# Two layers of a hybrid attention and mLSTM block on one core: another way to make the low parts of the mixers' weight pieces

## The chip, the core and the metric

The kernel runs on one core of a Trainium2 chip. The core has TensorE (matrix products), VectorE, ScalarE, GpSimd and SyncE, each with its own queue of instructions that it takes in order, and 16 DMA engines that all queues share. The metric is the device time of one execution in microseconds, as a median of several runs.

## What is computed

Two layers, each a mixer and a feed-forward part over 512 positions of width 1024. The mixer projects the normalized input to eight groups of columns, runs dilated attention on three of them and a bidirectional mLSTM on the others, and projects the result back. Everything is float32.

```python
def hybrid_mixer(hn, w_in, mlstm_conv_w, mlstm_conv_b, mlstm_gate_b, mlstm_head_g, w_out):
    ...
    aq, ak, av, mq, mk, mv, mo, gates = jnp.split(hn @ w_in, split_at, axis=-1)
    ...
    attn = dilated_attention(q, k, v)
    ...
    qk = jax.nn.silu(depthwise_conv_centred(jnp.concatenate([mq, mk], axis=-1), mlstm_conv_w, mlstm_conv_b))
    ...
    h_fwd = mlstm_direction(q, k, v, g[0], jax.nn.log_sigmoid(g[1]))
    h_bwd = flip(mlstm_direction(flip(q), flip(k), flip(v), flip(g[2]), flip(jax.nn.log_sigmoid(g[3]))))
    ...
    return jnp.concatenate([attn, mlstm], axis=-1) @ w_out

def reference(x, ...):
    for l in range(DEPTH):
        mixed = hybrid_mixer(rms_norm(x, mix_pre_g[l]), w_in[l], ...)
        x = x + rms_norm(mixed, mix_post_g[l])
        ff = conv_ffn(rms_norm(x, ffn_pre_g[l]), w_up[l], ...)
        x = x + rms_norm(ff, ffn_post_g[l])
    return x
```

## The kernel before

**Products in three parts.** A large product is not made in plain float32. Both operands are split into a high part, rounded to float32r, and a low part, the rest. Each product is then a triple of matmuls: high weight by high input, low weight by high input, high weight by low input (`mac`, lines 230 to 232). Where the weights move through the array instead (the V columns), the triple stands in lines 923 to 925.

**Pieces.** The weights come in pieces of 128 x 8 x 128 numbers, 512 KB. A layer has 104: 28 of `w_in` (numbered 0 to 27 here), 8 of `w_out`, 44 of `w_up`, 24 of `w_down`. `plan` lists them in the order of use. `load_raw` lets SyncE load the next piece into one of three raw buffers (`RAW`). `split_w` then makes the two parts in the next buffers of two rings of three (`RING`): line 183 lets ScalarE write the high part `whi`, and `lo_part` (line 115) lets VectorE subtract it from the raw piece and write the low part `wlo`; then the next load is issued. Some pieces get other places (`alloc`), those of `w_in` never. A buffer of a ring is free when TensorE has read the piece three before for the last time. `prefetch` splits up to two pieces ahead of the one in use.

**Rounds of the mixer.** `w_in` is worked off in four rounds and a tail; `ORDER` gives the letters of each round: q and k are the mLSTM's projections, a and b the attention's, V a pair of pieces for the V columns of both, used together by `proj_v` (first sister for four of eight blocks, the second for the other four, for each of four chunks of positions). The pieces are: round one q 0, k 1, a 2, V 3 and 4, b 5; round two a 6, q 7, b 8, k 9, V 10 and 11; round three q 12, k 13, V 14 and 15, a 16, b 17; round four q 18, a 19, b 20, k 21, V 22 and 23; tail 24 to 27. Between the matmuls of the projections, two streams interleave the steps of attention (`attn`) and of the mLSTM (`mlstm`): scores on TensorE, a maximum on VectorE (line 749), exp and scaling on ScalarE (752, 754), transposes on TensorE (760), the split of the transposed weights on ScalarE and VectorE (763, 115), the product with V (786).

**What sets the order.** The program is written in one order, and a scheduler then orders the instructions of each engine by its own estimates of when each can start. A change of one instruction thus moves others.

At the start of a mixer the scale of the rows is made (`scale_ready`): VectorE computes it, TensorE spreads it, ScalarE copies it to `prow` (line 394), VectorE multiplies the tables (`tb`, 538 and 539) and the first projections (`cu`, 664) by it.

Of the kernel before, what the change touches and what calls it, by code (L numbers as in the profile page):

```python
# [11 lines left out]
AF = mybir.ActivationFunctionType  # L12
ALU = mybir.AluOpType
# [12 lines left out]
RAW = 3  # L26
LINE = 256
RING = 3
HD = 128
KSC = HD ** -0.5  # L30
SUM1, ROW1, SUM2, ROW2 = [int(t * 2400) for t in (0.6, 3.3, 2, 8)]
# [50 lines left out]
def tile_hybrid_block(ctx: ExitStack, tc: tile.TileContext, xt, w_in, w_g, w_out, w_up, w_down, par, cst, out):  # L82
    nc = tc.nc
# [6 lines left out]
    base = const  # L90
    wraw_p, whi_p, wlo_p = Lines(big, small, RAW), Lines(big, small, RING), Lines(big, small, RING)
    pp = pool("pp", space=PSUM)
# [21 lines left out]
    def lo_part(dst, src, hi):  # L114
        nc.vector.tensor_tensor(out=dst, in0=src, in1=f32v(hi), op=ALU.subtract)  # L115
# [50 lines left out]
    def split_w(alloc=None):  # L166

        if not raw_q:
            return None
        raw, nk, i = raw_q.popleft()  # L170
        parts = {}
        n = 8
        k = 0
        while k < nk:
            if alloc is None:

                o = 16 if i in moving else 0
                hi, lo = (q.tile([P, 8 * P + LINE // 4], F32R, tag=t, name=t)[:, o:o + 8 * P].rearrange("p (k c) -> p k c", k=8)
                          for q, t in ((whi_p, "whi"), (wlo_p, "wlo")))
            else:  # L180
                hi, lo, n = alloc()
            m = min(n, nk - k)
            nc.scalar.copy(out=hi[:, 0:m, :], in_=raw[:, k:k + m, :])  # L183
            lo_part(lo[:, 0:m, :], raw[:, k:k + m, :], hi[:, 0:m, :])
            for j in range(m):
                parts[k + j] = (hi[:, j, :], lo[:, j, :])
            parts["all"] = (hi, lo)
            k += m
        load_raw()
        return parts  # L190
# [285 lines left out]
    def mixer_first(l, xp, sp, G, more, whole=False):  # L476
# [23 lines left out]
        if more:  # L500
            scale.go(1)
            w = take()
            prefetch(RING - 1)
            ps = s_ps()
# [6 lines left out]
    def mixer(l, xp, first, mp, post):  # L511
# [377 lines left out]

        prefetch(RING - 1)  # L890
        scale_ready()
# [5 lines left out]
        def proj():  # L897
            if pss:
                return pss.pop(0)
            w = take()  # L900
            prefetch(RING - 1)
            ps = mm_ps()
# [102 lines left out]
        for m in range(G):  # L1005
            mac(pss[m], ws[m], order[7], cp[order[7]], False, True)
        prefetch(RING)
        for m in range(G):
# [6 lines left out]
        for m in range(G, KT - 2):  # L1015
            w = take()
            ps = o_ps() if m == G else mm_ps()
            prefetch(RING if m == G else RING - 1)
            for n, k in enumerate(order):
# [262 lines left out]
```

## Time and profile before

| | us |
|---|---|
| median of 3 runs (1354.68 to 1354.85) | 1354.69 |
| the profiled execution | 1353.89 |
| its span in the profile | 1352.0 |
| first mixer, from the start of the span | about 25 to 262 |
| second mixer | about 697 to 930 |

The profile is of one execution; its span runs from the first to the last instruction, and the rest of its 1353.89 us lies around it. Times in its rows are from the start of the span. A row of a timeline gives start, duration, engine, line, operation, output and inputs, and in brackets idle time before it with what ended that. In a table by stretch each engine's busy time stands with its number of instructions.

### The profile page before, as it was taken

To read this page: it belongs to the slowest core of one execution; us is meant where nothing else is said; L and a number is where in the kernel's file an instruction comes from. 1 tells how busy PE (TensorE), PEld (TensorE's weight loads), DVE (VectorE), ACT (ScalarE), POOL (GpSimd) and SP (SyncE) were. 2 spreads that over 40 slices of the span, in tenths; PEclk is the share of its full clock that TensorE was granted. 3 is DMA by queue.
4 is the path that set the end of the run, shared out by engine and by line. 5 is a ranking of instruction groups with operands and counts; after the bars stand their busy time and mean duration, and the time that the engine had idled before them with its cause. 6 is when DMAs were issued, how large, how long until landed. Compare 5 with 4: busy or idle time off the path is not lost.

```text
span 1352.0 us, 18666 instructions
## 1 busy us (share of the span) xinstructions
PE 1323.9 (98%) x7152; PEld 1128.6 (83%) x7152; DVE 954.0 (71%) x1901; ACT 713.1 (53%) x1218; POOL 85.3 (6%) x100
## 2 busy tenths in 40 slices
PE   7999999999999999999989999999999999999996
PEld 5888878899888888888978898888998888888886
DVE  6999798847887777422499988887569777773233
ACT  5686696654544444323347867966446444443220
POOL 0000000024000000001130000000320000000002
PEclk9999999999999999999999999999999999999998
DMA  6212112231233332333321122123213333333321
GB/s 238 63 41 86 47 48 79 78 126 44 68 107 96 104 97 90 90 97 111 96 85 51 60 64 65 45 79 99 90 47 96 106 95 94 94 96 96 98 86 63
DMA packets 34089, 115.34 MB, mean 85 GB/s; under 512 B 3664, under 2 KB 6352, under 8 KB 34000
## 3 DMA queue, kind: packets, MB, share of 16 engines
q1 hardware_dynamic: 34000, 114.15, 27.9%
q8 instruction: 56, 0.92, 0.3%
q14 instruction: 33, 0.27, 0.1%
HBM read 112.04 MB, written 2.10 MB: 84 GB/s over the span
## 4 chain that ended last, share of the span: by engine, by line
PE 85%; DVE 7%; ACT 7%; issue 1%; DMA 0%; POOL 0%; SPq 0%; ACTq 0%; DVEq 0%
PE mm L230 18%; PE mm L232 18%; PE mm L231 18%; PE o L230 5%; PE o L231 5%; PE o L232 5%; PE mm L924 2%; PE mm L925 2%; PE mm L923 2%; PE o L786 2%; ACT rb L707 1%; PE t L760 1%; PE t L344 1%; DVE wlo L115 1%; ACT p L752 1%; PE s L743 1%
## 5 line engine op out<-in xcount | busy, mean ns | idle before, releaser
L115 DVE TENSOR_TENSOR wlo<-wraw,whi 128x1024 fp32r<-128x1024 f32 (+1 forms) x192 | 236.5, 1234 | 175.4 <-ACT whi L183 173.3
L230 PE MATMUL mm<-ah,whi 128*128 128x512 f32 (+1 forms) x880 | 337.0, 383 | 0.0
L232 PE MATMUL mm<-al,whi 128*128 128x512 f32 (+1 forms) x880 | 333.2, 380 | 0.8 <-DVE al L378 0.7
L231 PE MATMUL mm<-ah,wlo 128*128 128x512 f32 (+1 forms) x880 | 333.3, 379 | 0.0
L183 ACT CAST whi<-wraw 128x1024 fp32r<-128x1024 f32 (+1 forms) x192 | 198.0, 1035 | 163.2 <-PE mm L232 112.3
L232 PEld LDWEIGHTS mm<-al,whi 128*128 128x128 f32 x880 | 166.2, 189 | 30.8 <-DVE al L378 1.6
L230 PEld LDWEIGHTS mm<-ah,whi 128*128 128x128 f32 x880 | 166.5, 189 | 28.8 <-ACT whi L183 0.5
L231 PEld LDWEIGHTS mm<-ah,wlo 128*128 128x128 f32 x880 | 166.6, 189 | 27.3
L326 POOL TENSOR_TENSOR acc<-acc,sq 128x512 f32<-128x512 f32 x22 | 29.5, 1342 | 1127.0 <-ACT sq L323 1122.6
L230 PE MATMUL mm<-hh,whi 128*128 128x512 f32 x220 | 85.6, 389 | 0.0
L231 PE MATMUL mm<-hh,wlo 128*128 128x512 f32 x220 | 85.6, 389 | 0.0
L232 PE MATMUL mm<-hl,whi 128*128 128x512 f32 x220 | 85.6, 389 | 0.0
L1059 DVE TENSOR_TENSOR u<-mm,prow 128x512 f32<-128x512 f32 x64 | 43.8, 687 | 50.0 <-PE mm L232 39.6
L1076 ACT CAST hh<-cv 128x512 fp32r<-128x512 f32 x44 | 27.3, 620 | 87.6 <-DVE cv L1073 87.6
L923 PE MATMUL mm<-whi,ah 128*128 128x256 f32 x256 | 72.4, 284 | 0.9 <-DVE cu L664 0.9
L924 PE MATMUL mm<-wlo,ah 128*128 128x256 f32 x256 | 71.7, 280 | 0.4 <-DVE wlo L115 0.4
L925 PE MATMUL mm<-whi,al 128*128 128x256 f32 x256 | 71.4, 279 | 0.0
L1071 ACT ACTIVATE cg<-cg 128x512 f32<-128x512 f32 x44 | 27.8, 632 | 74.6 <-DVE cg L1065 74.3
L231 PE MATMUL o<-ah,wlo 128*128 128x512 f32 (+1 forms) x160 | 60.6, 379 | 0.0
L232 PE MATMUL o<-al,whi 128*128 128x512 f32 (+1 forms) x160 | 60.5, 378 | 0.0
L230 PE MATMUL o<-ah,whi 128*128 128x512 f32 (+1 forms) x160 | 60.5, 378 | 0.0
L752 ACT ACTIVATE p<-p,mx 128x512 f32<-128x512 f32 x64 | 46.2, 722 | 18.2 <-DVE mx L749 16.9
(319 smaller groups left out, 2754.9 us busy)
## 6 DMA issues: line engine op xcount, KB each, us to landing
wraw<-in_w_up SPq DMA_DIRECT2D x88, 512.0 KB, 3.6
wraw<-in_w_in SPq DMA_DIRECT2D x56, 512.0 KB, 3.6
wraw<-in_w_down SPq DMA_DIRECT2D x32, 512.0 KB, 3.5
wraw<-in_w_out SPq DMA_DIRECT2D x16, 512.0 KB, 3.6
wraw<-in_w_down SPq DMA_DIRECT2D x16, 384.0 KB, 3.1
x<-in_xt SPq DMA_DIRECT2D x4, 512.0 KB, 7.3
out_dram<-x SPq DMA_DIRECT2D x8, 256.0 KB, 2.1
tb<-in_cst SPq DMA_DIRECT2D x2, 967.0 KB, 5.4
```

The lines of the kernel that those rows point to most:

```text
L115: nc.vector.tensor_tensor(out=dst, in0=src, in1=f32v(hi), op=ALU.subtract)
L183: nc.scalar.copy(out=hi[:, 0:m, :], in_=raw[:, k:k + m, :])
L230: nc.tensor.matmul(out=ps, lhsT=hi, rhs=rh, start=first, stop=False)
L231: nc.tensor.matmul(out=ps, lhsT=lo, rhs=rh, start=False, stop=False)
L232: clock[1] = nc.tensor.matmul(out=ps, lhsT=hi, rhs=rl, start=False, stop=last).ins
L326: e.tensor_tensor(out=self.acc[:, cols], in0=self.acc[:, cols], in1=sq, op=ALU.add)
L752: nc.scalar.activation(out=p_, in_=p_, func=AF.Exp, scale=-1.0, bias=mx, accum_out=den)
L923: nc.tensor.matmul(out=o_, lhsT=xh, rhs=hi, start=(k == 0), stop=False)
L924: nc.tensor.matmul(out=o_, lhsT=xh, rhs=lo, start=False, stop=False)
L925: clock[1] = nc.tensor.matmul(out=o_, lhsT=xl, rhs=hi, start=False, stop=(k == KT - 1)).ins
L1059: nc.vector.tensor_tensor(out=u, in0=ps, in1=st["row"], op=ALU.mult)
L1071: nc.scalar.activation(out=g, in_=g, func=AF.Gelu_apprx_tanh)
```

## The change

For 52 pieces, those of `w_in` in both layers without the first four of layer 0, the low part is made in another way: ScalarE writes minus the raw piece, rounded like the high part, into the buffer of the low part (line 187 of the new code), and then GpSimd issues a DMA (188) that reads the raw piece and the buffer, adds them and writes the sum to the buffer. VectorE has no part in it. The write needs the raw piece and the free buffer, not the high part, so it may stand ahead of the cast. All other pieces are split as before. What waited for VectorE's subtraction (TensorE's second matmul, the next load into the raw buffer) now waits for the DMA's landing.

```diff
@@ -26,6 +26,7 @@
 RAW = 3
 LINE = 256
 RING = 3
+PIECES = 104
 HD = 128
...
             m = min(n, nk - k)
             nc.scalar.copy(out=hi[:, 0:m, :], in_=raw[:, k:k + m, :])
-            lo_part(lo[:, 0:m, :], raw[:, k:k + m, :], hi[:, 0:m, :])
+            if alloc is None and i % PIECES < 28 and i > 3:
+
+                nc.scalar.activation(out=lo[:, 0:m, :], in_=raw[:, k:k + m, :], func=AF.Copy, scale=-1.0)
+                nc.gpsimd.dma_start(out=lo[:, 0:m, :], in_=raw[:, k:k + m, :], accum_op=ALU.add)
+            else:
+                lo_part(lo[:, 0:m, :], raw[:, k:k + m, :], hi[:, 0:m, :])
             for j in range(m):
```

Lines from 188 on lie 6 higher in the new code: L713 there is L707 here. The numbers behind names are those of buffers and differ between the two programs.

**ScalarE, fourth round of layer 0.** `whi_8619` before and `whi_8666` now are piece 23. Before:

```order
L763 CAST pth_8509<-t_8511 128x4x128
L752 ACTIVATE p_8502,den_8505<-p_8502,mx_8503 128x512
L707 COPY rb_8603<-mm_8556 32x512
L183 CAST whi_8619<-wraw_8219 128x1024
L754 ACTIVATE p_8502<-p_8502,den_8505 128x512
L183 CAST whi_8661<-wraw_8327 128x1024
L763 CAST pth_8509<-t_8518 128x4x128
L886 COPY cat6_8594<-t_8589 128x512
```

Now:

```order
L769 CAST pth_8555<-t_8564 128x4x128
L892 COPY cat6_8641<-t_8636 128x512
L713 COPY rb_8650<-mm_8603 32x512 x3
L796 COPY cat2_8280<-o_8536 64x512
L184 CAST whi_8666<-wraw_8264 128x1024
L187 ACTIVATE wlo_8667<-wraw_8264 128x1024
L184 CAST whi_8709<-wraw_8373 128x1024
L673 ACTIVATE ca_8700<-cu_8698,par1_67 128x512
```

The cast now stands behind the last attention copies, which stood behind it, and the write of minus the raw piece follows it. From the cast of piece 20 to that of piece 23, ScalarE has 51 instructions between before and 58 now: three writes of minus the raw piece, one L754, one L763, one L790 and one L886 more.

**TensorE, the V pair 22 and 23 of layer 0.** `wlo_8551` and `wlo_8620` before are the low parts of 22 and 23, `wlo_8597` and `wlo_8667` now; `mm` is the chunk pair's sum. Before:

```order
L923 MATMUL mm_8667<-whi_8550,ah_6248 128x256
L924 MATMUL mm_8667<-wlo_8551,ah_6248 128x256
L786 MATMUL o_8490<-pth_8509,vs_8062 128x256 x4
L925 MATMUL mm_8667<-whi_8550,al_6249 128x256
L923 MATMUL mm_8667<-whi_8619,ah_6257 128x256
L924 MATMUL mm_8667<-wlo_8620,ah_6257 128x256
```

Now:

```order
L931 MATMUL mm_8716<-whi_8596,al_6276 128x256
L929 MATMUL mm_8716<-whi_8666,ah_6284 128x256
L929 MATMUL mm_8765<-whi_8596,ah_6250 128x256
L930 MATMUL mm_8765<-wlo_8597,ah_6250 128x256
L931 MATMUL mm_8765<-whi_8596,al_6251 128x256
L929 MATMUL mm_8765<-whi_8596,ah_6257 128x256
```

and, eight rows on,

```order
L931 MATMUL mm_8765<-whi_8596,al_6276 128x256
L929 MATMUL mm_8765<-whi_8666,ah_6284 128x256
L236 MATMUL mm_8838<-ah_6250,whi_8709 128x512
L930 MATMUL mm_8716<-wlo_8667,ah_6284 128x256
L931 MATMUL mm_8716<-whi_8666,al_6285 128x256
```

The first use of the low part of 23 now stands behind all four triples of the second chunk with piece 22, one more high-part matmul and the first matmul of piece 24.

**VectorE, start of the mixer of layer 1.** `wlo_6628` is the low part of piece 4; that of piece 3 stands four rows ahead of the rows shown. Before:

```order
L115 TENSOR_TENSOR wlo_6628<-wraw_6061,whi_6627 128x1024
L296 SCALAR_TENSOR_TENSOR rs_y_6588<-rs_a_6589,rs_y_6588 128x2
L551 TENSOR_TENSOR G_6647<-t_6642,G_6647 128x64
L395 TENSOR_SCALAR rt_6329<-rs_y_6588 128x2
L552 TENSOR_TENSOR G_6647<-G_6647,rt_6329 128x64
```

Now:

```order
L302 SCALAR_TENSOR_TENSOR rs_y_6616<-rs_a_6617,rs_y_6616 128x2
L530 CAST bdm_6588<-tb_6584 64x512
L401 TENSOR_SCALAR rt_6356<-rs_y_6616 128x2
L544 TENSOR_TENSOR tb_6584<-tb_6584,prow_6357 128x512
L545 TENSOR_TENSOR tb_6584<-tb_6584,prow_6357 128x512
L670 TENSOR_TENSOR cu_6633<-mm_6354,prow_6357 128x512
```

Both subtractions are gone, and the work on the gates (`G`) stands behind the tables and `cu`.

## Rows read from the trace of the kernel before

**Rows 1.** Page, busy time of each engine: us, share of the span, instructions.

```profile
PE 1323.9 (98%) x7152; PEld 1128.6 (83%) x7152; DVE 954.0 (71%) x1901; ACT 713.1 (53%) x1218; POOL 85.3 (6%) x100
```

**Rows 2.** Busy time in both mixers: length, PE, PEld, DVE, ACT, POOL, clock, DMA, GB/s.

```profile
25.00:262.00 237.00, 233.92 (x1428) 201.21 (x1428) 211.64 (x535) 172.77 (x340) 0.13 (x1) 1.00 0.22 63
697.00:930.00 233.00, 230.46 (x1413) 198.14 (x1412) 209.61 (x520) 171.49 (x339) 0.00 (x0) 1.00 0.22 64
```

**Rows 3.** TensorE's waits in both mixers: total us, times, longest.

```profile
PE s L864 <- DVE r L871: 0.7, 1, 0.7
PE s L864 <- DVE hs L874: 0.5, 1, 0.5
PE t L760 <- ACT p L754: 0.4, 2, 0.2
...
PE mm L923 <- DVE cu L664: 0.9, 1, 0.9
PE s L743 <- DVE mx L749: 0.3, 1, 0.3
```

**Rows 4.** First mixer by line: busy us, mean ns, idle before, what ended it.

```profile
L115 DVE TENSOR_TENSOR wlo<-wraw,whi 128x1024 fp32r<-128x1024 f32 x28 | 34.2, 1221 | 3.4 <-ACT whi L183 3.3
...
L183 ACT CAST whi<-wraw 128x1024 fp32r<-128x1024 f32 x28 | 29.1, 1046 | 9.1 <-PE mm L925 4.8 <-PE mm L232 4.2
```

**Rows 5.** Timelines of VectorE and TensorE at the start of layer 1's mixer.

```profile
699.21 1.22 DVE L115 TENSOR_TENSOR wlo<-wraw,whi 128x1024 fp32r<-128x1024 f32 x1
...
702.98 1.28 DVE L664 TENSOR_TENSOR cu<-mm,prow 128x512 f32<-128x512 f32 x2
...
703.81 0.36 PE L923 MATMUL mm<-whi,ah 128*128 128x256 f32 x1 [0.86 <-DVE cu L664]
```

**Rows 6.** Busy time from the cast of piece 20 to that of 23, both layers.

```profile
167.30:201.50 34.20, 33.74 (x181) 27.19 (x181) 30.94 (x85) 30.90 (x65) 0.00 (x0) 1.00 0.19 58
835.80:870.00 34.20, 33.77 (x181) 27.21 (x181) 30.91 (x85) 30.89 (x64) 0.00 (x0) 1.00 0.18 57
```

**Rows 7.** ScalarE in that stretch of layer 0: timeline, and groups by line.

```profile
170.50 1.06 ACT L183 CAST whi<-wraw 128x1024 fp32r<-128x1024 f32 x1 [1.47 <-PE mm L232]
...
201.53 1.05 ACT L183 CAST whi<-wraw 128x1024 fp32r<-128x1024 f32 x1
...
L754 ACT ACTIVATE p<-p,den 128x512 f32<-128x512 f32 x7 | 4.9, 710 | 0.0
...
L763 ACT CAST pth<-t 128x512 fp32r<-128x512 f32 x7 | 4.0, 582 | 0.1
```

**Rows 8.** Page: a load's count, size, us to landing; the queue's packets, MB, share.

```profile
wraw<-in_w_in SPq DMA_DIRECT2D x56, 512.0 KB, 3.6
...
q1 hardware_dynamic: 34000, 114.15, 27.9%
```

**Rows 9.** Timelines of VectorE and TensorE around piece 23 in layer 0.

```profile
202.75 1.22 DVE L115 TENSOR_TENSOR wlo<-wraw,whi 128x1024 fp32r<-128x1024 f32 x1
...
201.39 0.40 PE L230 MATMUL mm<-ah,whi 128*128 128x512 f32 x1
201.62 0.40 PE L231 MATMUL mm<-ah,wlo 128*128 128x512 f32 x1
...
205.50 0.28 PE L923 MATMUL mm<-whi,ah 128*128 128x256 f32 x1
205.62 0.28 PE L924 MATMUL mm<-wlo,ah 128*128 128x256 f32 x1
```

**Rows 10.** Timelines of ScalarE, VectorE and TensorE around piece 11 in layer 0.

```profile
91.75 2.00 ACT L183 CAST whi<-wraw 128x1024 fp32r<-128x1024 f32 x2
...
97.78 1.22 DVE L115 TENSOR_TENSOR wlo<-wraw,whi 128x1024 fp32r<-128x1024 f32 x1
...
99.05 0.39 PE L924 MATMUL mm<-wlo,ah 128*128 128x256 f32 x1 [0.20 <-DVE wlo L115]
```

**Rows 11.** Busy time of 25 us between the layers.

```profile
675.00:700.00 25.00, 21.72 (x153) 19.29 (x153) 22.43 (x61) 12.25 (x29) 12.56 (x17) 0.93 0.18 55
```

## The prediction

> **What bounds the kernel now.** I read the engines' line of the page first. TensorE shows matmuls in 98% of the span; VectorE is busy 954.0 us, ScalarE 713.1 us, GpSimd 85.3 us [rows 1]. A busy TensorE may still be waiting inside that figure, so the next view is busy time by stretch. The two mixers lie at 25 to 262 and 697 to 930 us. There TensorE has 237.00 - 233.92 = 3.1 us and 233.00 - 230.46 = 2.5 us without a matmul, 5.6 us together, while VectorE is busy 89% and 90%, ScalarE 73% and 74%, GpSimd not at all [rows 2]. So the mixers are bound by TensorE, with VectorE close behind. The waits say what those gaps are: in the first mixer VectorE ends the named ones of 0.7, 0.5 and three of 0.2 us, in the second 0.9, 0.3 and two of 0.2 us; ScalarE ends 0.4 and 0.2 us in each, beside 1.1 us at the second's very start [rows 3]. What a freed VectorE can return is therefore small: 1.8 + 1.6 = 3.4 us by name, 5.6 us if every gap closed. Since matmul rows overlap (0.39 us long, 0.23 apart, [rows 9]), short waits can hide in busy time; I let the far bound be twice the gaps, 11 us.
>
> **What is removed.** 24 subtractions in layer 0 (pieces 4 to 27 of its 28) and 28 in layer 1 leave VectorE: 52 x 1.22 us = 63 us [rows 4]. Hardly any of it lies on the path, by the waits above. One place does: at the start of layer 1's mixer a subtraction of 1.22 us stands in VectorE's queue at 699.21, ahead of the scale row's work and of `cu` at 702.98, for which TensorE waits 0.86 us [rows 5]. The order shows both subtractions gone from there; the 0.86 us are in the 3.4. Gain taken: 3.4 us, bounds 0 and 11.
>
> **What is added on ScalarE.** 52 writes of minus the raw piece. The trace has no such row, but the cast of the same piece by the same engine takes 1.05 us [rows 4]: 52 x 1.05 = 55 us. Averaged over the mixers this fits (73% becomes about 85%); stage by stage it does not. From the cast of piece 20 to that of piece 23 ScalarE is busy 30.90 of 34.20 us, and 30.89 of 34.20 us at the same place of layer 1, with VectorE at 30.9 as well [rows 6]. In the order of the changed kernel ScalarE has seven more instructions between these two casts: three of the new writes (3.1 us), one L754 (0.71 us) and one each of L763, L790 and L886, copies of one size that take 0.58 us [rows 7], 2.4 us for the four, which the scheduler put ahead of the cast because it counts on an earlier VectorE. That is 5.5 us into 3.3 us of idle time: the cast of piece 23, at 201.53 us now, moves back 2.2 us if all idle time is used and 5.5 us if none is. I take 3.0 us, near the lower end, because the longest idle piece (1.47 us, [rows 7]) was a wait for TensorE that other work can now fill.
>
> **What is added on GpSimd and the DMA engines.** 52 transfers that read 512 KB of raw piece and 512 KB of low part and write 512 KB. Call L the time from the end of ScalarE's write to the landing. No such transfer is in the trace. The nearest row is a load of 512 KB from HBM, 3.6 us from issue to landing; the queue moved 114.15 MB in 27.9% of the span, so the bytes of one load take 1.73 us [rows 8]. A second pass for the part that is read back makes 3.6 + 1.7 = 5.3 us, my value; the ends are 3.6 us (the second pass hidden) and 7.2 us (everything doubled). The Trainium skill (DMA: Bandwidth & Descriptors, section Anatomy of one DMA) gives a plain transfer issued by GpSimd as 2.0 us plus its bytes over 436 GB/s, which is an estimate of 3.2 us here, and with that the sum below would come out near +0.4 us, no change; no transfer issued by GpSimd is in this trace. GpSimd's queue is empty in the mixers [rows 2]; behind each transfer's wait stand only later transfers, small memsets, and in layer 1's first three pieces the residual additions, whose operands are made only after those pieces are split. SyncE's next load of a raw piece now waits for the transfer instead of for VectorE, L - 1.2 = 4 us later; casts in the mixer wait for TensorE alone (4.8 and 4.2 us), never for a load [rows 4], so that is covered. The cost if the cover goes is one load, 3.6 us.
>
> **Where the longer way is not covered.** The low part is needed by the second matmul of each triple. Most pieces are split 10 to 20 us ahead. The tight ones are second V pieces, which share the ring of three with their sister.
>
> Piece 23 (fourth round): the cast starts at 201.53, VectorE's subtraction at 202.75 lasts 1.22, and TensorE uses the low part at 205.62 [rows 7, 9]; spare time 1.7 us. Now: cast at 204.5, done 205.6, minus the raw piece done 206.6, landed 206.6 + 5.3 = 211.9. TensorE's order delays the use: twelve more V matmuls (0.12 apart), one more high-part matmul and one projection matmul (0.23) stand ahead, 1.4 + 0.1 + 0.2 = 1.8 us [rows 9], so it arrives at 207.4. It waits 4.5 us. Bounds: shift 2.2 and L 3.6 give 2.0 us; shift 5.5 and L 7.2 give 8.9 us. In layer 1 the same: 9.0 us together.
>
> Piece 11 (second round): ScalarE casts it at 91.75, and VectorE, crowded, subtracts only at 97.78; TensorE waits for it at 99.05 [rows 10]. Now: cast done 92.8, one 0.5 us instruction, write done 94.4, landed 99.7: 0.6 us later than now, twice 1.2 us; bounds by L -1.1 and +2.5 each. So here the transfer merely takes the place of the crowded engine.
>
> Piece 6 and the other pieces behind a V pair (13, 17, 25) have 8.4 to 10.8 us between the release of their buffer and their use, counted in the new order at 0.12 us a V matmul and 0.23 us a projection matmul, against 1.05 + 1.05 + 5.3 = 7.4 us: nothing at my L, 1 to 2 us each at 7.2 us.
>
> One more cost is bounded and not in the sum. From 675 to 700 us, where TensorE is busy 21.72 of 25.00 us, the granted clock averages 0.93 [rows 11]: part of that stretch ran at 1.2 GHz, 1.75 us lost. A wait of 4.5 us could do the same, 0 to 1.75 us per layer; I take 0 because that stretch has several idle spells, not one.
>
> **Sum.** -3.4 + 9.0 + 1.2 = +6.8 us. On the profiled execution, 1353.89 us with a span of 1352.0, that is 1360.7; the median of the runs is 0.8 us above the profiled one, so 1361.5 us.
>
> **Rivals.**
> Faster: ScalarE's idle time takes up nearly all the new work, the transfer lands in about 3.6 us as a load does, and relief of VectorE reaches the waits hidden in busy time. Then piece 23 costs about 2 us a layer and piece 11 gains 1: -8 + 4 - 2 = -6, some 1349 us. For it: VectorE at 90% in both mixers, and the subtraction of piece 11 came 4 us late behind it. Against it: TensorE names only 3.4 us of waits for VectorE.
> No change: L about 4 us, the late piece costs 2.5 us a layer, the gain is 3.4 to 5: within 2.7 us of 1354.7.
> Much slower: adding in the DMA engines is far slower than a second pass, L 9 us or more. The decisive point is about 7.5 us: above it the pieces behind V pairs are late too. At 9 us pieces 23 and 11 cost 8.2 and 4.3 us a layer and some four more pieces 2 us each, 41 us less the gain: about 1392 us; at 7.5 us about 1371.
>
> **How the numbers follow.** 0.2% is 2.7 us, about what a measurement of this kernel can tell from no change. Forecast (slower through ScalarE's crowded stretch and the late piece, 1357.5 to 1368 us): 0.50. Faster: 0.25. No change: 0.18. Much slower: 0.07. Time: 1361.5. The range takes in most of the faster case and the bounds of the late piece with the clock, 1347.5 to 1373; the tail above and the best of the faster case stay out. Cases of both signs hold most of the chance; the forecast's own range is the 1357.5 to 1368 above. Faster by over 0.2%: 0.25; within: 0.18; slower: 0.57.
>
> **What would show it.** Right: in the profile after, TensorE's largest new wait is for the transfer at piece 23, around 207 and 875 us, of 2 to 9 us; ScalarE is nearly solid from the cast of piece 20 to that of piece 23; VectorE falls by about 63 us; `cu` no longer holds TensorE near 703 us; the transfers land 4 to 7 us after ScalarE's write. Wrong: L below 4 us, or no idle spell of TensorE near 207 us, or a gain spread over many small gaps in rounds one and two, which would mean that busy time hid more waiting for VectorE than the waits name.

## The result, and the profile after

The change makes the kernel slower: 1370.48 us median (1368.74 to 1371.57, 4 runs) against 1354.77 for the kernel before, a ratio of 1.0114 with a 95% interval of 1.010 to 1.0128. That is +15.7 us; the forecast was +6.8. The sign and the first suspect were right, the size was less than half. The profiled execution of after took 1371.57 us, its span 1369.8, so the traces differ by 17.8 us.

From the page of the kernel after: busy time of the engines, the new queue's packets, MB and share of 16 engines, the two new instructions, and the new transfer with its median from issue to landing. They answer to [rows 1, 4, 8].

```profile
PE 1328.3 (97%) x7152; PEld 1131.5 (83%) x7152; DVE 907.1 (66%) x1849; ACT 758.2 (55%) x1270; POOL 130.9 (10%) x152
...
q0 software_dynamic: 7488, 27.27, 10.5%
...
L188 POOL DMA_DIRECT2D wlo<-wraw x52 | 45.5, 874 | 418.2 <-ACT wlo L187 242.5
...
L187 ACT ACTIVATE wlo<-wraw 128x1024 fp32r<-128x1024 f32 x52 | 54.9, 1056 | 38.8 <-PE mm L237 23.0
...
wlo<-wraw POOLq DMA_DIRECT2D x52, 512.0 KB, 4.8
```

VectorE has lost 46.9 us of busy time, ScalarE has gained 45.1 and GpSimd 45.6. The write of minus the raw piece costs 1056 ns, as the cast did. Busy time in both mixers, to be read against [rows 2] (same stretches, same columns):

```profile
25.00:262.00 237.00, 229.28 (x1404) 196.93 (x1404) 184.71 (x495) 189.08 (x354) 21.23 (x25) 0.99 0.48 114
697.00:930.00 233.00, 220.86 (x1345) 189.68 (x1343) 175.67 (x466) 182.06 (x334) 23.91 (x29) 0.98 0.51 121
```

TensorE has 7.7 and 12.1 us without a matmul where it had 3.1 and 2.5, and the granted clock is no longer 1.00. What it waited for, over the whole run (total us, times, longest):

```profile
PE mm L930 <- DMA wlo<-wraw: 9.4, 5, 2.7
PE mm L490 <- ACT ah L383: 8.4, 3, 7.0
PE s L365 <- DVE rs_y L302: 6.5, 5, 2.0
PE s L749 <- ACT ak L728: 2.2, 3, 1.0
PE t L587 <- issue: 1.2, 1, 1.2
PE mm L236 <- ACT gs L549: 1.0, 1, 1.0
```

The first row is new. Its five waits are timeline rows of TensorE, all of them at the first use of the low part of a *second* V sister: piece 4 of layer 0, then 11 and 23 of both layers.

```profile
35.89 0.38 PE L930 MATMUL mm<-wlo,ah 128*128 128x256 f32 x1 [0.87 <-DMA wlo<-wraw]
100.55 0.38 PE L930 MATMUL mm<-wlo,ah 128*128 128x256 f32 x1 [1.61 <-DMA wlo<-wraw]
211.79 0.38 PE L930 MATMUL mm<-wlo,ah 128*128 128x256 f32 x1 [2.71 <-DMA wlo<-wraw]
781.57 0.39 PE L930 MATMUL mm<-wlo,ah 128*128 128x256 f32 x1 [1.56 <-DMA wlo<-wraw]
892.85 0.58 PE L930 MATMUL mm<-wlo,ah 128*128 128x256 f32 x1 [2.69 <-DMA wlo<-wraw]
```

The row for `rs_y` had 4.6 us in four waits before and has a fifth of 1.9 us now; the row for `gs` is new. Both stand at the start of layer 1's mixer. ScalarE there (first fence, after) and TensorE (second):

```profile
700.49 1.06 ACT L187 ACTIVATE wlo<-wraw 128x1024 fp32r<-128x1024 f32 x1 [0.33 <-PE mm L237]
701.46 1.03 ACT L184 CAST whi<-wraw 128x1024 fp32r<-128x1024 f32 x1
702.39 0.36 ACT L400 COPY prow<-s 128x256 f32<-128x256 f32 x1
702.65 1.04 ACT L184 CAST whi<-wraw 128x1024 fp32r<-128x1024 f32 x1
703.60 1.06 ACT L187 ACTIVATE wlo<-wraw 128x1024 fp32r<-128x1024 f32 x1
704.55 0.36 ACT L400 COPY prow<-s 128x256 f32<-128x256 f32 x1
704.81 0.57 ACT L549 COPY gs<-mm 32x512 f32<-32x512 f32 x1
```

```profile
701.32 0.50 PE L350 MATMUL t<-mean,sqql 128*128 128x1 f32 x4
703.74 0.68 PE L365 MATMUL s<-ident_rs,rs_y 128*128 128x128 f32 x4 [1.91 <-DVE rs_y L302]
705.43 0.80 PE L236 MATMUL mm<-ah,whi 128*128 128x512 f32 x1 [1.01 <-ACT gs L549]
```

In the kernel before, the copy of the gate sums `gs` was ScalarE's first work there and piece 2's projection followed the sums at once; only then came the second row product (L359, now L365). The rows of before:

```profile
695.29 0.57 ACT L543 COPY gs<-mm 32x512 f32<-32x512 f32 x1 [0.69 <-PE mm L486]
695.77 1.04 ACT L183 CAST whi<-wraw 128x1024 fp32r<-128x1024 f32 x1
```

```profile
695.77 0.50 PE L344 MATMUL t<-mean,sqql 128*128 128x1 f32 x4
696.13 0.49 PE L230 MATMUL mm<-ah,whi 128*128 128x512 f32 x1
...
700.72 0.60 PE L359 MATMUL s<-ident_rs,rs_y 128*128 128x128 f32 x4
```

From the sums to the first matmul of the projection it was 0.36 us and is 4.11 us. Last, the clock. Three stretches of after by the view of busy time by stretch (the third number from the end is the granted clock; 0.50 is 1.2 of 2.4 GHz):

```profile
213.20:216.60 3.40, 3.40 (x19) 3.40 (x17) 0.69 (x1) 0.44 (x1) 0.10 (x1) 0.50 0.97 264
704.70:711.50 6.80, 6.07 (x16) 4.47 (x17) 6.27 (x10) 2.41 (x5) 0.86 (x1) 0.50 0.96 199
892.40:895.80 3.40, 2.95 (x14) 2.96 (x15) 2.27 (x4) 1.34 (x2) 0.87 (x1) 0.50 0.60 160
```

The first begins 1.4 us behind the end of the wait for piece 23 in layer 0, the third in the last 0.4 us of that in layer 1, and the second in the wait for `gs` at layer 1's start. The stretch of 3.4 us at half clock between the layers that lay in [rows 11] is there in both kernels. So this execution has 13.6 us more at half clock, 6.8 us of work lost at most (less, where TensorE would have waited anyway).

### The profile page after: what moved, and what is told of

Same layout as the page of the kernel before. It is cut to its first block, busy times and chain, and to the rows that moved or that the text cites. A ratio compares the mean times of both kernels' runs of the same rounds, so it can differ in the third digit from the quotient of the medians.

```text
span 1369.8 us, 18786 instructions
## 1 busy us (share of the span) xinstructions
PE 1328.3 (97%) x7152; PEld 1131.5 (83%) x7152; DVE 907.1 (66%) x1849; ACT 758.2 (55%) x1270; POOL 130.9 (10%) x152
## 3 DMA queue, kind: packets, MB, share of 16 engines
q0 software_dynamic: 7488, 27.27, 10.5%
## 4 chain that ended last, share of the span: by engine, by line
PE 85%; ACT 5%; DVE 4%; issue 3%; DMA 2%; POOL 0%; SPq 0%; POOLq 0%; ACTq 0%
PE mm L236 18%; PE mm L238 18%; PE mm L237 18%; PE o L236 5%; PE o L238 5%; PE o L237 5%; PE mm L930 2%; PE mm L931 2%; PE mm L929 2%; DMA wlo<-wraw 2%; PE t L766 2%; PE o L792 2%; PE s L749 1%; PE s L750 1%; ACT rb L713 1%
## 5 line engine op out<-in xcount | busy, mean ns | idle before, releaser
L116 DVE TENSOR_TENSOR wlo<-wraw,whi 128x1024 fp32r<-128x1024 f32 x140 | 172.9, 1239 | 162.0 <-ACT whi L184 160.2
L188 POOL DMA_DIRECT2D wlo<-wraw x52 | 45.5, 874 | 418.2 <-ACT wlo L187 242.5
L187 ACT ACTIVATE wlo<-wraw 128x1024 fp32r<-128x1024 f32 x52 | 54.9, 1056 | 38.8 <-PE mm L237 23.0
```

The source lines that it names most:

```text
L187: nc.scalar.activation(out=lo[:, 0:m, :], in_=raw[:, k:k + m, :], func=AF.Copy, scale=-1.0)
L188: nc.gpsimd.dma_start(out=lo[:, 0:m, :], in_=raw[:, k:k + m, :], accum_op=ALU.add)
```

## Where the time goes, by stage

The same matmuls are compared in both traces: the first sums of mixer 0's end (293.80 us before), the last sums of layer 0 (688.32), the first matmul of the first and of the last V triple of layer 1's first pair (703.81 and 714.83), the sums of mixer 1's end (961.84). The delay that each stage adds, in us, in the profiled execution of the change and of each run told of below:

| | mixer 0 | start of mixer 1, to the end of its first V pair | rest of mixer 1 | median against before |
|---|---|---|---|---|
| the change | +5.6 | +4.9 | +7.7 | +15.7 |
| a_hi_for_lo | +0.3 | -0.6 | +1.5 | +0.3 |
| g_plain_copy | +0.6 | -0.8 | +1.5 | +0.9 |
| b_no_dma | +0.8 | +4.2 | +3.2 | +8.3 |
| i_vector_adds | +1.3 | +4.1 | +2.4 | +8.2 |
| e_not_11_23 | +1.1 | +4.1 | +3.5 | +6.8 |
| m_only_11_23 | -0.4 | 0.0 | +4.1 | +3.5 |
| k_write_first | +3.4 | +2.4 | +5.9 | +13.7 |
| d_late_start | +4.3 | +1.3 | +6.6 | +12.2 |
| l_only_start | -0.3 | +4.9 | +2.2 | +5.7 |
| f_both | +0.9 | +1.9 | +1.2 | +2.9 |
| n_gs_first | +5.3 | +4.0 | +7.7 | +16.0 |
| p_gs_first_not_4 | +6.5 | -0.4 | +6.3 | +10.3 |
| q_sisters | +0.3 | +0.2 | +1.8 | +1.2 |
| r_before_gs | 0.0 | +0.3 | +0.4 | +0.3 |

Up to 1 us can lie ahead of mixer 0 (the first loads) and is in no column. The feed-forward parts, which were not changed, add or take 0.5 us at most. The last column is a difference of medians; single executions of one kernel differ by up to 5 us where waits and half clock vary.

## Experiments: what each part of the change costs by itself

My theory after the result had three parts: late transfers at second V sisters, ScalarE's writes ahead of the gate sums at the start of layer 1, and a clock that falls behind such waits. The rival for each was that the part named only lands last. The edits are shown against the changed kernel.

**a_hi_for_lo**: the freed VectorE with nothing put in place of its work.

```diff
-                nc.scalar.activation(out=lo[:, 0:m, :], in_=raw[:, k:k + m, :], func=AF.Copy, scale=-1.0)
-                nc.gpsimd.dma_start(out=lo[:, 0:m, :], in_=raw[:, k:k + m, :], accum_op=ALU.add)
+                lo = hi
```

> VectorE's relief alone: for the 52 pieces nothing makes a low part, and the second matmul of each triple reads the high part instead, so the low part is left out of the result; no write of ScalarE and no transfer is added. Theory (the 15.7 us of the change come from late transfers, ScalarE's place at the start of layer 1's mixer, and the clock behind those waits): none of them is left, and the waits for VectorE return; 1351 to 1354 us, against 1354.8 before. Rival (the scheduler's new order, which follows from the lighter VectorE, costs time by itself): 1357 to 1362 us.

Measured: 1355.08 us (1354.12 to 1356.39), ratio 1.0004 (0.9995 to 1.0013): +0.3 us, with -0.7 to +1.8 for the interval. That is above the theory's range and below the rival's: the 3.4 us do not return, and the new order costs nothing measurable either. TensorE's longest waits in the first mixer of this run:

```profile
PE t L586 <- DVE lf L582: 1.0, 1, 1.0
PE s L748 <- ACT ak L727: 0.8, 2, 0.5
PE t L890 <- DVE hs L886: 0.6, 1, 0.6
PE o L791 <- ACT pth L768: 0.6, 3, 0.2
```

The longest waits named in [rows 3] are gone, and others stand in their place under the new order: with the shorter ones they come to 4.1 us for VectorE in both mixers, against 3.4 before. The longest, for `lf`, ends a chain of small steps, and VectorE's rows show no gap above 0.04 us from 42.84 us to the end of that chain at 46.19, with subtractions of 0.69 us for other work between the steps. So there is less work on VectorE in the mixer, but not in front of this wait. This run also bounds the idea: even a low part that costs nothing gains nothing here, 0.7 us at the interval's end, under the order that the scheduler makes.

**b_no_dma**: the write without the transfer.

```diff
-                nc.gpsimd.dma_start(out=lo[:, 0:m, :], in_=raw[:, k:k + m, :], accum_op=ALU.add)
```

> ScalarE's write alone: minus the raw piece is written into the low part as in the change, but nothing is added to it, so the low part is left at minus the raw piece. Theory (late transfers): the 9.4 us that TensorE waits for transfers and some 3.4 us of half clock behind them (213 and 892 us) go, the start of layer 1's mixer (+4.9 us) stays; 1357 to 1361 us. Rival (ScalarE's 55 us of writes are the cause, the transfer only lands last): 1364 to 1370 us.

Measured: 1363.12 us (1361.38 to 1364.28), ratio 1.0062 (1.0049 to 1.0074). Neither: +8.3 us, 2 us above the theory's upper end and just under the rival's range. ScalarE's writes by themselves are half of the loss, and the transfers add the other 7.4.

**i_vector_adds**: the same writes, and VectorE adds in place of the DMA.

```diff
-                nc.gpsimd.dma_start(out=lo[:, 0:m, :], in_=raw[:, k:k + m, :], accum_op=ALU.add)
+                nc.vector.tensor_tensor(out=lo[:, 0:m, :], in0=raw[:, k:k + m, :], in1=f32v(lo[:, 0:m, :]), op=ALU.add)
```

> ScalarE's writes as in the change, but VectorE adds the raw piece to them in place of the DMA: VectorE keeps all its 52 instructions, no transfer is added. Theory (ScalarE's writes cost their 8 us at the start of layer 1's mixer and in its second round whatever VectorE does, and the freed VectorE was worth nothing): 1361 to 1364 us, as without the DMA. Rival 1 (a lighter VectorE did hide part of the writes' cost): 1365 to 1369 us. Rival 2 (the loss at that start comes from the order that a lighter VectorE gives, not from ScalarE's writes): 1355 to 1358 us.

Measured: 1362.76 us (1361.74 to 1362.99), ratio 1.0058 (1.0046 to 1.0071). The theory's range: ScalarE's writes cost 8.2 us although VectorE is as busy as before. The start of layer 1 is hurt here too, by a fifth wait for `rs_y`:

```profile
PE s L365 <- DVE rs_y L302: 7.8, 5, 3.2
```

The second row product stands directly behind the sums, as in the change. So ScalarE's writes bring this order about, not the lighter VectorE.

**g_plain_copy**: no write, and a DMA that copies instead of adding.

```diff
-                nc.scalar.activation(out=lo[:, 0:m, :], in_=raw[:, k:k + m, :], func=AF.Copy, scale=-1.0)
-                nc.gpsimd.dma_start(out=lo[:, 0:m, :], in_=raw[:, k:k + m, :], accum_op=ALU.add)
+                nc.gpsimd.dma_start(out=lo[:, 0:m, :], in_=raw[:, k:k + m, :])
```

> A plain copy in place of ScalarE's write and the adding transfer: GpSimd's DMA copies the raw piece into the low part's buffer and nothing is subtracted, so the low part is left out of the result. It gives the price of the adding by itself. Theory (the adding costs a second pass, some 1.7 us, as the forecast had it): issue to landing about 3.1 us against 4.8 us in the change. Rival (the adding is free, the 4.8 us are those of any transfer of this size that GpSimd issues): 4.5 to 5 us. The time, without ScalarE's writes and with a transfer that starts as soon as the raw piece and the buffer are there: 1354 to 1357 us by both.

Measured: 1355.48 us (1353.97 to 1355.84), ratio 1.0005 (0.9996 to 1.0014). From its page:

```profile
q0 software_dynamic: 7488, 27.27, 5.5%
...
L187 POOL DMA_DIRECT2D wlo<-wraw x52 | 27.8, 534 | 407.6 <-PE mm L237 205.8
...
wlo<-wraw POOLq DMA_DIRECT2D x52, 512.0 KB, 2.9
```

Issue to landing is 2.9 us against 4.8: adding costs 1.9 us, near the 1.7 us of a second pass that the forecast put on. The same 27.27 MB keep the DMA engines busy 5.5% of their time instead of 10.5%. The Trainium skill (DMA: Bandwidth & Descriptors, section Anatomy of one DMA) gives 2.0 us plus the bytes over 436 GB/s, an estimate of 3.2 us; the plain copy's 2.9 us agrees with that, and the adding transfer does not follow it.

## Experiments: where it costs

**e_not_11_23**: pieces 11 and 23 stay with VectorE.

```diff
-            if alloc is None and i % PIECES < 28 and i > 3:
+            if alloc is None and i % PIECES < 28 and i > 3 and i % PIECES not in (11, 23):
```

> The change for all of its pieces but the second sisters 11 and 23 of both layers, which stay with VectorE. Theory (late second sisters): their waits of 1.9, 1.8, 2.7 and 2.7 us go, and with those of piece 23 the two stretches at half clock of 3.4 us (1.7 us lost in each); 9.1 + 3.4 = 12.5 us at most, of which something comes back as waits for VectorE; 1358 to 1363 us. Rival (the delay is of the whole round, other pieces become late in their place): 1366 to 1370 us.

Measured: 1361.58 us (1361.00 to 1362.62), ratio 1.0052 (1.0040 to 1.0065): 9.0 us less than the change, within the theory's range. Of TensorE's waits for transfers one of 0.7 us is left. (The waits at piece 11 that go are of 1.6 us each, by the rows above, not the 1.9 and 1.8 of the expectation.) With 48 of the 52 pieces still changed, the kernel is 6.8 us slower than before; the four second sisters made up the other 9.0.

**m_only_11_23**: the same four pieces alone are changed (`i % PIECES in (11, 23)`).

> The change for pieces 11 and 23 of both layers alone; all other pieces stay with VectorE. Theory 1 (the transfer itself is too long for piece 23, even where ScalarE is not crowded by other writes): by the rows of before, cast of piece 23 done at 202.6, write at 203.6, landed 5.2 later at 208.8, used at 205.6, so 3.2 us of wait, twice, with or without half clock behind it, and nothing at piece 11; 1360 to 1363 us. Theory 2 (it is the other writes that push ScalarE's cast of piece 23 back): 0 to 2 us, 1354.5 to 1357 us.

Measured: 1358.16 us (1357.56 to 1358.84), ratio 1.0026 (1.0016 to 1.0035): +3.5 us, between the two. The trace splits it. Piece 23 is not late at all: the write is made 12 us ahead of the cast, since it needs only the raw piece and the buffer (ScalarE's timeline of this run, layer 0):

```profile
191.77 1.06 ACT L187 ACTIVATE wlo<-wraw 128x1024 fp32r<-128x1024 f32 x1
...
203.36 1.05 ACT L184 CAST whi<-wraw 128x1024 fp32r<-128x1024 f32 x1
```

In the change the same write stands behind the cast:

```profile
204.85 1.05 ACT L184 CAST whi<-wraw 128x1024 fp32r<-128x1024 f32 x1
205.81 1.06 ACT L187 ACTIVATE wlo<-wraw 128x1024 fp32r<-128x1024 f32 x1
```

This run leaves out ScalarE's other writes, but it also leaves VectorE its other subtractions. i_vector_adds tells the two apart: it has all 52 writes and a VectorE as busy as before, and there the write of piece 23 is early too:

```profile
190.99 1.06 ACT L187 ACTIVATE wlo<-wraw 128x1024 fp32r<-128x1024 f32 x1
...
203.40 1.05 ACT L184 CAST whi<-wraw 128x1024 fp32r<-128x1024 f32 x1
```

In b_no_dma, with the writes and a lighter VectorE, it stands behind the cast again, at 206.09. So neither the transfer nor ScalarE's other writes alone put it there; in these runs it comes late only where ScalarE has the writes and the scheduler orders them beside a lighter VectorE.

Piece 11, by contrast, is waited for even alone (TensorE, both layers):

```profile
99.18 0.39 PE L930 MATMUL mm<-wlo,ah 128*128 128x256 f32 x1 [1.46 <-DMA wlo<-wraw]
...
770.93 0.58 PE L930 MATMUL mm<-wlo,ah 128*128 128x256 f32 x1 [1.90 <-DMA wlo<-wraw]
```

There the way over the transfer is too long: from the write's end to the landing it takes 4.9 and 4.8 us. The cost is layer 1's: by the table mixer 0 loses nothing (-0.4 us), since the low part lands at 99.13, hardly later than VectorE's subtraction ended before (99.00, [rows 10]), while the rest of mixer 1 loses 4.1 us, with 3.4 us at half clock from the end of the wait on. The reading of theory 1 on piece 23, made from rows of before, was wrong because it kept the write behind the cast; its reading of nothing at piece 11 was wrong too.

**k_write_first**: the write ahead of the cast for all pieces.

```diff
-            nc.scalar.copy(out=hi[:, 0:m, :], in_=raw[:, k:k + m, :])
             if alloc is None and i % PIECES < 28 and i > 3:
...
                 nc.gpsimd.dma_start(out=lo[:, 0:m, :], in_=raw[:, k:k + m, :], accum_op=ALU.add)
+                nc.scalar.copy(out=hi[:, 0:m, :], in_=raw[:, k:k + m, :])
             else:
+                nc.scalar.copy(out=hi[:, 0:m, :], in_=raw[:, k:k + m, :])
```

> The change with ScalarE's two instructions in the other order: minus the raw piece first, then the cast, so that each transfer starts about 1.05 us earlier and each high part is ready 1.05 us later. Theory (pieces 11 and 23 wait for the landing alone): about 1 us less of each of the four waits, 1366 to 1368 us, and one stretch at half clock fewer at best. Rival (the transfer's place is set by when ScalarE gets to the piece, and the later cast holds the first matmul of the triple by as much): 1369.5 to 1371.5 us.

Measured: 1368.31 us (1365.30 to 1369.67), ratio 1.0098 (1.0085 to 1.0112): 2.0 us less than the change. The waits for transfers sum to 7.6 us instead of 9.4, 0.7 us less at piece 23 and 0.1 at piece 11, in each layer: half of what was expected of an earlier start, and the time is 0.3 us above the theory's range. The profiled execution is the fastest of the four (1365.30 us; the others took 1367.50 to 1369.67) and shows something else: none of the stretches at half clock that the change added is in it, although its waits for piece 23 are 2.0 us. The same order at layer 1's start costs 2.4 us here, at full clock, against 4.9 with 6.8 us at half clock.

**d_late_start**: pieces 0 to 4 of layer 1 stay with VectorE.

```diff
-            if alloc is None and i % PIECES < 28 and i > 3:
+            if alloc is None and i % PIECES < 28 and i > 3 and not 104 <= i < 109:
```

> The change for all of its pieces but the first five of layer 1 (0 to 4), which stay with VectorE; the order at the start of layer 1's mixer is then that of before, the row product behind most of piece 2's projection. Theory (the order and ScalarE's writes at that start cost 4.9 us, with the half clock of 704.7 to 711.5 us among it): 1365 to 1366.5 us, and no stretch at half clock there. Rival (the lost time only moves to the next V pair, since the mixer is bound by the transfers further on): 1369 to 1371 us.

Measured: 1367.00 us (1366.23 to 1367.42), ratio 1.0091 (1.0076 to 1.0107): 3.5 us less than the change, the theory's direction and a little short of its range. The order at that start is that of before again, and no stretch near it is at half clock.

**l_only_start**: these five pieces alone are changed (`104 <= i < 109`).

> The change for the first five pieces of layer 1 alone (0 to 4); all other pieces stay with VectorE. Theory (these five by themselves cost what leaving them out gave back): 3.5 to 5.5 us, 1358 to 1360 us. Rival (the start of that mixer is hurt only because ScalarE and TensorE come to it late and crowded): at most 1.5 us, 1354.5 to 1356 us.

Measured: 1360.40 us (1357.86 to 1361.08), ratio 1.0036 (1.0022 to 1.0050): +5.7 us by the medians (3.0 to 6.8 by the interval), a little above the theory's range and clear of the rival's. The table has +4.9 at the start, as in the full change, and TensorE's waits there are the same 1.91 us for `rs_y` and 1.02 us for `gs`. The loss belongs to these pieces, not to a late arrival at the stage.

**f_both**: d and e together.

> The two edits of the runs d_late_start and e_not_11_23 together: the change for all of its pieces but 0 to 4 of layer 1 and 11 and 23 of both layers, which stay with VectorE. Theory (two separate losses that add up: 3.5 us at the start of layer 1's mixer, 8.9 us at the second sisters): 1357 to 1359 us, some 3 us above the kernel before, which is what ScalarE's other writes and piece 4 cost. Rival (the two places are one loss, since a delay at the start of a mixer is what makes its later pieces late): 1360.5 to 1362 us, no better than e_not_11_23.

Measured: 1357.49 us (1356.93 to 1358.43), ratio 1.0023 (1.0014 to 1.0032). The two losses add up: 3.5 + 9.0 = 12.5 us expected back, 15.7 - 2.9 = 12.8 measured.

## Experiments: the start of layer 1's mixer

**n_gs_first**: ScalarE's copy of the gate sums gets priority.

```diff
-            nc.scalar.copy(out=gs, in_=ps[0:32, :])
+            with tc.high_priority():
+                nc.scalar.copy(out=gs, in_=ps[0:32, :])
```

> The change as it is, but ScalarE's copy of the gate sums (gs) is given priority, so that it stands ahead of the writes of minus the raw piece and the casts at the start of layer 1's mixer, as it does in the kernel before; everything else is untouched. Theory (the loss at that start comes from the gate sums' copy behind ScalarE's writes: TensorE needs that buffer, and the scheduler moved the row product ahead for the same reason): 2.5 to 5 us less than the change, 1365.5 to 1368 us. Rival (the loss comes from ScalarE's time as such, whatever stands first): 1369.5 to 1371.5 us.

Measured: 1370.68 us (1370.34 to 1371.39), ratio 1.0117 (1.0103 to 1.0131). No gain: the time is the rival's, but the trace is not. The wait of 1.9 us for `rs_y` is gone, that for `gs` is 0.2 us, and to the layer's first V matmul the stage adds -0.3 us. Thirteen matmuls of the pair later TensorE stands still for another reason (timeline):

```profile
712.84 0.39 PE L931 MATMUL mm<-wlo,ah 128*128 128x256 f32 x1 [2.60 <-DMA wlo<-wraw]
```

That is piece 4, the second sister of the first V pair. TensorE comes to it 5.8 us earlier than in the change, and its low part lands 2.5 us later, at 712.79 instead of 710.28. Half a microsecond of that is the write, now behind `gs` and `prow` (from 704.09, in the change from 703.60); the other 2.0 us are the transfer, 7.6 us from the write's end instead of 5.6, with a raw piece's load and another adding transfer beside it.

**p_gs_first_not_4**: n, and piece 4 of layer 1 stays with VectorE (`i != 108`).

> The run n_gs_first (the change, with ScalarE's copy of the gate sums ahead of its writes) with one more edit: piece 4 of layer 1, the second sister of that mixer's first V pair, stays with VectorE. Theory (two late things stand one behind the other at that start: the gate sums' copy with the row product, and behind it the low part of piece 4; mending the first alone only showed the second, as the 2.6 us wait for a transfer at 710 us in n_gs_first says): 2.5 to 5 us less than the change, 1365.5 to 1368 us, and no wait of TensorE for a transfer near 710 us. Rival (a third thing takes their place, ScalarE's time there is simply too much): 1369 to 1371.5 us.

Measured: 1364.86 us (1362.31 to 1367.53), ratio 1.0076 (1.0064 to 1.0089): 5.5 us less than the change and 0.6 us below the theory's range. The stage costs nothing any more (-0.4). Two late things stood one behind the other, and mending the first only uncovered the second.

**q_sisters**: n, and the second sisters 4, 11 and 23 stay with VectorE (`i % PIECES not in (4, 11, 23)`).

> The change with ScalarE's copy of the gate sums ahead of its writes, and with the three second sisters whose transfers come late (4, 11 and 23 of both layers) left with VectorE; pieces 0 to 3 of layer 1 stay in the change, unlike in f_both. Theory (late second sisters and the place of the gate sums' copy are the whole loss but some 3 us): 1356.5 to 1359 us, as f_both. Rival (the first pieces of layer 1 cost time for a reason of their own): 1360.5 to 1363 us, as e_not_11_23.

Measured: 1355.83 us (1354.75 to 1357.29), ratio 1.0011 (1.0002 to 1.0020), 0.7 us below the theory's range: 46 of the 52 pieces made in the new way, and 1.2 us left of 15.7. Its busy times, and the waits at layer 1's start, where the rows for `rs_y` and transfers are missing:

```profile
PE 1321.0 (98%) x7152; PEld 1126.4 (83%) x7152; DVE 911.6 (67%) x1855; ACT 753.8 (56%) x1264; POOL 125.5 (9%) x146
```

```profile
PE mm L490 <- ACT ah L383: 1.1, 1, 1.1
PE mm L492 <- DVE al L384: 0.7, 1, 0.7
PE mm L236 <- ACT gs L550: 0.2, 1, 0.2
```

VectorE is 42.4 us lighter than before and the kernel is not faster, as a_hi_for_lo had it. So ScalarE's 49 us of writes cost next to nothing either, once TensorE waits for none of them.

**r_before_gs**: the priority for `gs` put into the kernel before, as a control.

> The kernel before, with ScalarE's copy of the gate sums given priority and nothing else, as a control for the three runs that use this edit. That copy stands ahead of the casts there already. Theory (the edit is worth nothing by itself): 1353.5 to 1355.5 us. Rival (it moves other work in the mixers and part of what p_gs_first_not_4 and q_sisters gave back is its own): 1351 to 1353 us, or slower than 1356.

Measured: 1354.79 us against 1354.51, ratio 1.0004 (0.9995 to 1.0013). The edit is worth nothing by itself; what p and q gave back is the change's own loss.

No version of the change measured here beats the kernel before, and a_hi_for_lo puts the worth of freeing VectorE alone at nothing, within 0.7 us, under the scheduler's order.

## Why the prediction was right and wrong, by its steps

Three steps failed, and they are most of the 8.9 us between 6.8 and 15.7: the gain from VectorE (taken as 3.4 us, nothing measured), the start of layer 1's mixer (taken as a gain of 0.86 us, part of the 3.4; a loss of 4.9 measured) and the clock (taken as nothing).

- **The gain from VectorE, -3.4 us: failed.** a_hi_for_lo gives +0.3 us. The step took waits named for VectorE as time that a lighter VectorE returns. Under the new order other waits of the same size took their place, the longest behind a stretch in which VectorE was still busy throughout.
- **The start of layer 1's mixer: wrong sign.** The step saw both subtractions leave VectorE there and counted the 0.86 us for `cu` as a gain. It looked at the queue that was relieved, not at ScalarE's, into which two writes had been put ahead of `gs`, nor at TensorE's, where the second row product had moved ahead of piece 2's projection. Measured: +4.9 us, shown to belong to these five pieces by d and l and mended by p. It is the largest part of what was missing. Up to 3.4 us of it are the clock's: in k_write_first the same order costs 2.4 us at full clock.
- **The clock, taken as 0 of 0 to 1.75 us per layer: failed.** The reason given, that one idle spell would not do it, fell: at piece 23 single waits of 2.7 us have half-clock stretches at or behind their ends in both layers. They do not always: d_late_start has a wait of 2.71 us at piece 23 of layer 0 and full clock behind it. The profiled execution has 13.6 us more at half clock; the four executions of the change show mean granted clocks of 0.991 to 0.994, and the slowest has the lowest.
- **ScalarE's crowding before piece 23: the number right, its cause not.** In the change ScalarE (fourth busy time) is nearly solid from the cast of piece 20 to that of 23, and the cast of 23 moved from 201.53 to 204.85, 3.3 us against 3.0 taken. Of these, 1.0 us was lost ahead of the stretch, and the stretch is 2.4 us longer than in [rows 6]. Here are this stretch in the change, in a_hi_for_lo (no write, lighter VectorE) and in i_vector_adds (all writes, VectorE as busy as before):

```profile
168.30:204.85 36.55, 34.98 (x195) 28.25 (x194) 29.55 (x83) 35.50 (x71) 2.61 (x3) 1.00 0.39 88
167.58:203.57 35.99, 35.24 (x194) 27.96 (x193) 29.28 (x82) 32.94 (x68) 0.00 (x0) 1.00 0.16 45
169.04:203.40 34.36, 33.85 (x185) 27.18 (x184) 31.11 (x85) 33.51 (x67) 0.00 (x0) 1.00 0.17 47
```

  Without any write it grows by 1.8 us, with all three writes and the load left on VectorE by 0.2. So most of the growth is the order that comes with a lighter VectorE, which the step had counted with 2.4 of its 5.5 us, and little is the writes, counted with 3.1. That 3.0 was near is partly luck.
- **The transfer's duration L, 5.3 us: right for the middle.** From the write's end to the landing the median is 5.2 us; piece 23 took 4.9 (206.87 to 211.75, forecast 211.9). But L is no one number: it goes from 4.7 to 8.9 us. From issue to landing, some 0.4 us less, the 18 transfers beside which the packets show no other data moving took 4.4 to 4.7 us; those above 7 us all overlap loads of raw pieces.
- **Piece 23, 4.5 us of wait: 2.7 us in each layer**, since TensorE came to it at about 208.9 and not 207.4. Round four's V pair began 3.5 us later than before, and in a_hi_for_lo, where nothing is late, it begins 2.9 us later too: the scheduler moved other work ahead of it. Then half clock added up to 1.7 us to that in each layer. The sum of both, 4.4, matches the forecast only by that accident.
- **Piece 11, 0.6 us: 1.6 us.** The cast began at 93.31, 1.6 us later than before, and the write ended at 95.61, not 94.4; TensorE stood still from 98.94.
- **Piece 4, taken as nothing: 0.9 us in layer 0**, where its transfer took 7.0 us from the write's end (28.82 to 35.85; with 5.3 us it would have landed ahead of TensorE), and 2.6 us in layer 1 as soon as it was no longer hidden (n_gs_first). Only the pieces behind V pairs and two of the four rounds' second sisters were examined.
- **Loads, GpSimd's queue, the other 46 pieces at nothing: right**, within the 1.2 us that q_sisters leaves.

Not every wait costs its length. At the end of round three's V pair of layer 0 the change is 1.0 us behind the kernel before, and a_hi_for_lo 0.8, although the change has waited 0.9 and 1.6 us for pieces 4 and 11 by then. At the end of round four's pair it is 5.8 us behind, and a_hi_for_lo 0.5. In layer 1 the same two places read 13.6 and 18.3 for the change, 1.3 and 1.3 for a_hi_for_lo. So the two late pieces 23, with the clock, cost most of what the second sisters cost.

Some figures beside the sum do not follow from the prediction's own terms. TensorE waited 0.2 us for piece 11 ([rows 10]), so an earlier landing could return 0.2 us a layer, not the 1.1 of its lower bound or the 1 of the faster case. At L 4 us piece 23 would wait 3.2 us by these terms, not 2.5; at the 3.2 us of the plain transfer the sum would be about +1.0, not +0.4. None of this moves the forecast.

Of the rivals, none was it. "Much slower" had its decisive point in L at 7.5 us; the median was 5.2, and the four transfers above 7.5 us held nothing up. Its 1371 us at that point lie beside the measured time by chance. The loss came from places; a slow transfer had a part at piece 4 alone. The tests named for the forecast held (new wait at piece 23, though at 212 and 893 us, ScalarE nearly solid, `cu` gone, landings 4 to 7 us after the write for 45 of 52) except one: VectorE fell by 46.9 us, not 63. The durations of its rows add up to 61 us less, near the 63; rows of one engine overlap their neighbours by some 0.1 us at each end, and busy time counts an overlap once.

What stays open: why the order beside a lighter VectorE puts the write of piece 23 so late, and what the change would cost under the order of before, which no run kept; how the clock's share of the 15.7 us splits off in the median, since the stretches vary from one execution to the next; and why round two of layer 1 costs 0.6 to 3.2 us even where no transfer is waited for there (i_vector_adds 0.6, a_hi_for_lo 1.9, b_no_dma 3.2).

## What to carry to other kernels

Before moving work off an engine, run the kernel with that work left out: if that gains nothing, a cheaper way of doing it has nothing to win there. Then run it with the new work added and the old load left in place: the two runs tell what the new work costs from what the scheduler's new order costs. When work is moved onto an engine, read what it now stands ahead of in that engine's queue at the start of each stage and at the second half of each pair that shares a ring; the average share of busy time says nothing there. And when a mended wait gives no gain, look for the wait that it was hiding before dropping the theory.

## What the runs showed of the hardware

- Adding in the DMA engines made a 512 KB transfer within SBUF take 4.8 us from issue to landing instead of 2.9 (medians; the fastest took 4.4 and 2.8), the engines' busy share 10.5% instead of 5.5% for the same bytes, and GpSimd's issue 874 ns instead of 534.
- The adding transfers of one execution (the change) took 4.4 to 8.5 us from issue to landing at one size. Those with no other data moving beside them took 4.4 to 4.7 us, and the slowest ran beside loads; that the loads are the cause is read from the trace, and no run tests it.
- In the mixers the granted clock fell to half for stretches of 3.4 or 6.8 us, in or up to 1.5 us behind waits of TensorE: of 2.7 us at piece 23, of 1.9 and 1.0 us one behind the other at layer 1's start, and in m_only_11_23 at 770.8 us in one of 1.90 us. But d_late_start had a wait of 2.71 us in layer 0, and k_write_first waits of 2.0 us and the same two at layer 1's start, at full clock. Which waits bring it about is not settled by these runs.
